# A mixture-of-experts layer whose experts are taken in an order ranked on the chip

## The chip, the cores and the metric

The kernel runs on one core of a Trainium2 chip. The metric is the device time of one execution in microseconds (us), as the median of several runs; lower is better.

## The reference, cut to what matters

One encoder layer for 256 tokens of width 1024. A first half (convolution branch, differential attention, output projection) makes the residual stream `x`; the second half, where the change lies, sends each token to 4 of 32 experts:

```python
h2 = rms_norm(x, norm2_g[l]) * (1.0 + scale2) + shift2
logits = (h2 @ w_router + b_router)            # 256 x 32
top_v, top_i = lax.top_k(logits, 4)
gates = jax.nn.softmax(top_v, axis=-1)
...
gu = xb @ w_gate_up[e] + b_gate_up[e]          # xb: the tokens of expert e, 1024 -> 2 x 1024
g, u = jnp.split(gu, 2, axis=-1)
g = jnp.minimum(g, 7.0); u = jnp.clip(u, -7.0, 7.0)
y = (u + 1.0) * (g * jax.nn.sigmoid(1.702 * g))
return y @ w_down[e] + b_down[e]               # 1024 -> 1024
...
x = x + gate2 * (sum over a token's experts of gate * output)
```

All is float32. An expert has 12 MB of weights, the 32 experts 384 MB; each weight is used once per execution. The experts get 256·4/32 = 32 tokens on average, but unevenly.

## The kernel before

**Places.** The second half is a loop over 32 places `e` (L1010 to L1065); before the change place `e` is expert `e`. An expert's first 64 tokens are its first pass. A second pass takes tokens 65 to 128 of an expert that has more than 64: its parts stand in `tc.If(n > 64)` blocks, with `n` the expert's count, which `count(e)` (L950) loads from the row `cnt` into registers of PE, ACT and DVE. Further passes, for more than 128, stand behind the loop and are skipped with this input.

**One place.** PE runs the gate half (`gate_up(PG, …)`, line L857, 4 weight chunks); then the If with `extra_gate` (L1018); the bias and the up half (4 chunks); the turning of the result and the gathering of the next pair's tokens; the If with `extra_up` (L1038); the adding of earlier outputs into `Y`; the next gate's bias; `down` (L898, 4 chunks); and the If with `extra_down` (L1064). The order in each engine's queue is the order written. DVE's L862 (`gp<-pg`) starts when a gate ends. DVE's L923 runs only in a second pass, in `extra_gate`.

**Tokens.** `pos` holds each token's position within each expert, `ge` its gate weight, `ehot` a one-hot matrix over experts that picks bias rows. `hots` and `extra_hot` (`hx`) turn columns of these into matrices that select tokens. All columns are picked by a constant `e`.

**Weights.** `expert_weights(e)` (L955) issues the loads on SP's queue, one `dma_start` for each chunk of 128x2048 floats (1 MB): 8 of `wgu` and 4 of `wdn` an expert. The chunks go around a ring of 19 buffers (8 + 7 + 4 of three pools), so chunk n waits until PE has finished with chunk n − 19. PE's last use of a chunk comes after the If of its part, since a second pass uses the same chunks: four become free after L1018, four after L1038, four after L1064. SP issues in order, up to 8 weight transfers underway at once.

```python
    pattern = [ringA] * 8 + [ringB] * 7 + [ringW] * 4
...
    def wchunk(src):
        t = wtile()
        nc.sync.dma_start(t, src)
        return t
```

**Place 0.** Weights are issued long ahead of the loop, while the routing is worked out. During place 0's gate the function `turn_gates` (step k = 6 of 8) transposes `ge` on PE (L1003) and copies it to `gT` (L1004).

Of the kernel before, what the change touches and what calls it, by code (L numbers as in the profile page):

```python
# [13 lines left out]
T = 256  # L14
NT = 2
# [16 lines left out]
def hybrid_layer(tc, xT_d, par_d, ada_d, win_d, wout_d, bgu_d, bdn_d, wgu_d, wdn_d, out_d):  # L32
# [771 lines left out]
    def hots(es, name, weight):  # L804
        hot = wk.tile([128, NT, 2, 64], F32, name=name)
        for t in range(NT):
            for i, e in enumerate(es):
                V.tensor_scalar(hot[:, t, i], iota[:, 0:64], pos[:, t, e:e + 1], weight(t, e),
                                op0=OP.is_equal, op1=OP.mult)
        return hot.rearrange("p a b c -> p a (b c)")  # L810

    def gate_hots(es):
        return hots(es, "hotg", lambda t, e: ge[:, t, e:e + 1])
# [29 lines left out]
    def bias(e, g, tag=None):  # L843
        P = ps_e.tile([128, 512], F32, name=tag or ("pg", "pu")[g])
        for n in range(2):
            o = g * 1024 + n * 512
            TE.matmul(P[64 * n:64 * n + 64], ehot[:, e:e + 1].to_broadcast([96, 64]), b3[:, o:o + 512],
                      start=True, stop=False)
        return P
# [53 lines left out]
    def extra_hot(e, b):  # L903
        hot = wk.tile([128, NT, 64], F32, name="hx")
        for t in range(NT):
            V.tensor_scalar(hot[:, t], iota[:, 64 * b:64 * b + 64], pos[:, t, e:e + 1], r2[:, t:t + 1],
                            op0=OP.is_equal, op1=OP.mult)
        return hot

    def extra_gate(e, b, W, hot):  # L910
        xg = more2.rearrange("p (k s) -> p k s", k=KD)
        for q, tag in enumerate(("misc", "pd")):
            px = ps_e.tile([128, 4, 64], F32, name=tag)
            for i in range(4):
                k = 4 * q + i
                for t in range(NT):
                    TE.matmul(px[:, i], xtok[:, t, k * 128:k * 128 + 128], hot[:, t], start=t == 0, stop=t == NT - 1)
            for i in range(4):
                affine(xg[:, 4 * q + i], px[:, i], 4 * q + i)

        hg = more1.rearrange("p (t c s) -> p t c s", t=NT, c=2)
        for t in range(NT):
            V.tensor_scalar(hg[:, t], iota[:, None, 64 * b:64 * b + 64].to_broadcast([128, 2, 64]),  # L923
                            pos[:, t, e:e + 1], ge[:, t, e:e + 1], op0=OP.is_equal, op1=OP.mult)
        act_g(gate_up(bias(e, 0), xg, W), more3)
# [5 lines left out]
    def extra_up(e, W):  # L931
        xg = more2.rearrange("p (k s) -> p k s", k=KD)
        act_u(gate_up(bias(e, 1, "misc"), xg, W), more3, more3)
# [10 lines left out]
    def extra(e, b, W, D):  # L944
        extra_gate(e, b, W[0:4], extra_hot(e, b))
        extra_up(e, W[4:8])
        extra_down(D)

    def count(i, engines=(ET.PE, ET.Activation, ET.DVE)):
        return nc.values_load(cnt[0:1, i:i + 1], engines=engines, min_val=0, max_val=2 * T,  # L950
                              skip_runtime_bounds_check_because="a count of tokens")
# [27 lines left out]
    Y = [ps_y.tile([128, 2, T], F32, name=f"y{i}") for i in range(4)]  # L979
    prep_hot(0)  # L980
# [29 lines left out]
    for e in range(NE):  # L1010
# [160 lines left out]
```

## Time and profile before

| | |
|---|---|
| median of 3 runs | 1149.2 us (1148.97 to 1150.4) |
| the profiled execution's own time | 1154.69 us |
| its span in the profile | 1152.9 us |
| PE busy | 1074.8 us (93% of the span) |
| DVE, ACT, POOL busy | 337.9 (29%), 161.0 (14%), 24.8 (2%) |

The profile shows one execution, taken by the hardware profiler. Its page cuts the span into 40 slices of 28.8 us. A clock column gives the granted TensorE clock as a share of 2.4 GHz. "Busy" PE means that a matmul is in the array, not that the array is at its peak. A window row gives for one stretch its length, each engine's busy time with its count of instructions (PE, PE's weight loads, DVE, ACT, POOL), the mean granted clock, the DMA engines' busy share and the GB/s moved. A timeline row gives start, duration, engine, line, operation, what it writes <- what it reads, and in brackets the idle time before it with what ended that. SPq is SP's queue of DMA issues.

### The profile page before, as it was taken

How to read it: one execution, taken by the hardware profiler on the slowest of the kernel's cores; microseconds unless marked ns; L12 is line 12 of the kernel's file. 1: busy time of each engine (PE TensorE's matmuls, PEld its weight loads, DVE VectorE, ACT ScalarE, POOL GpSimd, SP SyncE). 2: the span in 40 equal slices, each digit the busy share in tenths (PEclk: the TensorE clock that was granted, in tenths of full speed). 3: DMA queues.
4: the chain of work that ended last, by engine and by line, in shares of the span. 5: the costliest groups of instructions: out<-in, count | busy, mean ns of one | idle time of the engine just before them, and what ended most of it. 6: DMA issues, size and time to landing. Idle time of an engine off the chain costs nothing. (4 is left out here: it accounts for less than half of the span.)

```text
span 1152.9 us, 13876 instructions
## 1 busy us (share of the span) xinstructions
PE 1074.8 (93%) x5404; PEld 489.7 (42%) x5409; DVE 337.9 (29%) x837; ACT 161.0 (14%) x333; POOL 24.8 (2%) x54
## 2 busy tenths in 40 slices
PE   8999999999999999999999999998988888898996
PEld 6645774444433444433444444443333333333333
DVE  4897762222221222221222222221222221211212
ACT  2343521101110010100101111010101000000100
POOL 0160000000000000000000000000000000000000
PEclk9999999999999999999999999999999999999999
DMA  9999589999997999977999999999999999999994
GB/s 371 395 349 358 211 308 421 418 419 420 418 422 291 396 419 420 420 296 290 408 420 419 420 418 419 420 419 420 419 420 420 420 420 419 419 420 420 419 405 152
DMA packets 65428, 448.59 MB, mean 389 GB/s; under 512 B 7744, under 2 KB 7744, under 8 KB 11808
## 3 DMA queue, kind: packets, MB, share of 16 engines
q1 hardware_dynamic: 63856, 445.27, 94.4%
q8 instruction: 83, 1.36, 0.5%
q0 software_dynamic: 1456, 1.69, 0.5%
q14 instruction: 33, 0.27, 0.1%
HBM read 444.33 MB, written 1.05 MB: 386 GB/s over the span
## 5 line engine op out<-in xcount | busy, mean ns | idle before, releaser
L857 PE MATMUL pu<-w,xg 128*64 128x512 f32 x1024 | 233.5, 596 | 20.1 <-DMA w<-in_wgu_dram 19.9
L857 PE MATMUL pg<-w,xg 128*64 128x512 f32 x1024 | 232.5, 597 | 12.6 <-DMA w<-in_wgu_dram 7.4
L898 PE MATMUL pd<-w,yT 128*64 128x512 f32 x992 | 218.1, 592 | 0.0
L857 PEld LDWEIGHTS pg<-w,xg 128*64 128x64 f32 x1024 | 79.4, 136 | 159.8 <-issue 139.0
L857 PEld LDWEIGHTS pu<-w,xg 128*64 128x64 f32 x1024 | 76.4, 136 | 154.8 <-issue 99.5
L898 PEld LDWEIGHTS pd<-w,yT 128*64 128x64 f32 x992 | 69.6, 137 | 127.9 <-issue 124.2
L862 DVE TENSOR_SCALAR gp<-pg 128x512 f32<-128x512 f32 x34 | 23.5, 692 | 218.7 <-PE pg L857 218.7
L1061 DVE COPY o<-pd 64x512 f32<-64x512 f32 x31 | 21.2, 683 | 226.4 <-PE pd L898 226.4
L871 DVE TENSOR_SCALAR gp<-pu 128x512 f32<-128x512 f32 x32 | 22.1, 692 | 169.8 <-issue 164.2
L840 PE MATMUL y<-s,o 128*128 128x256 f32 x256 | 64.0, 390 | 4.0
L824 PEld LDWEIGHTS misc<-hot,xtok 128*128 128x128 f32 x496 | 57.9, 192 | 12.4 <-issue 12.2
L824 PE MATMUL misc<-hot,xtok 128*128 128x128 f32 x496 | 62.1, 278 | 0.0
L217 DVE SCALAR_TENSOR_TENSOR w<-w,crow 128x1024 f32<-128x1024 f32 x48 | 56.8, 1220 | 12.7 <-DMA w<-in_ada_dram 12.7
L840 PEld LDWEIGHTS y<-s,o 128*128 128x128 f32 x256 | 45.7, 189 | 20.9 <-issue 16.1
L1063 ACT ACTIVATE o<-pd 64x512 f32<-64x512 f32 x31 | 18.4, 594 | 256.2 <-DVE o L1061 256.2
L865 ACT ACTIVATE sg<-gp 128x512 f32<-128x512 f32 x32 | 20.2, 631 | 234.5 <-DVE gp L862 234.5
L404 PE MATMUL pq<-w,hT 128*128 128x512 f32 x96 | 42.7, 596 | 0.0
L882 ACT ACTIVATE yT<-pu 128x256 f32<-128x256 f32 x32 | 12.3, 384 | 175.0 <-PEq L1038 164.7
L800 ACT ACTIVATE xg<-misc,modT,a 128x128 f32<-128x128 f32 x62 | 28.4, 458 | 43.2 <-DVE xg L802 43.2
L270 PE MATMUL cv<-hT,w 128*128 128x256 f32 x128 | 30.2, 397 | 3.4 <-DMA w<-in_win_dram 3.4
L643 PE MATMUL pq<-mixT,w 128*128 128x256 f32 x128 | 29.3, 382 | 1.5 <-DVE xT L699 1.5
L802 DVE TENSOR_SCALAR xg<-misc,a,modT 128x128 f32<-128x128 f32 x62 | 25.2, 406 | 18.3 <-ACT xg L800 16.4
(308 smaller groups left out, 680.1 us busy)
## 6 DMA issues: line engine op xcount, KB each, us to landing
w<-in_wgu_dram SPq DMA_DIRECT2D x256, 1024.0 KB, 19.9
w<-in_wdn_dram SPq DMA_DIRECT2D x124, 1024.0 KB, 19.9
w<-in_ada_dram SPq DMA_DIRECT2D x24, 1024.0 KB, 13.8
w<-in_win_dram SPq DMA_DIRECT2D x10, 1024.0 KB, 12.7
w<-in_wout_dram SPq DMA_DIRECT2D x4, 1024.0 KB, 10.9
w<-in_wdn_dram SPq DMA_DIRECT2D x8, 512.0 KB, 14.4
w<-pad POOLq DMA_DIRECT2D x32, 35.5 KB, 6.2
xT<-in_xT_dram SPq DMA_DIRECT2D x4, 256.0 KB, 9.9
```

Of the source, the lines that this page charges most:

```text
L217: V.scalar_tensor_tensor(w, w, 1.0, crow, op0=OP.mult, op1=OP.mult, accum_out=modT[:, s, 2 * q + i:2 * q + i + 1])
L270: TE.matmul(pcv[j][:, g], WI[0, q][:, o:o + 128], hT[:, k], start=k == 0 and g == 0, stop=k == KD - 1, skip_group_check=True)
L404: TE.matmul(PQ[w, t], hT[:, k, t * 128:t * 128 + 128], WI[1 + w, k // 4][:, (k % 4) * 512:(k % 4) * 512 + 512], start=k == 0, stop=k == KD ...
L643: TE.matmul(po4[d // 2][:, d % 2], WO[i][k // 2][:, o:o + 128], mixT[:, 4 * i + k], start=first and k == 0 and d % 2 == 0, stop=last and k ...
L800: A.activation(dst, src, AF.Identity, scale=a2[:, k:k + 1], bias=sh2[:, k:k + 1])
L802: V.tensor_scalar(dst, src, a2[:, k:k + 1], sh2[:, k:k + 1], op0=OP.mult, op1=OP.add)
L824: TE.matmul(px[:, i], xtok[:, t, k * 128:k * 128 + 128], PP[p][:, t], start=t == 0, stop=t == NT - 1)
L840: TE.matmul(Y[d // 2][:, d % 2], O[p][:, d * 128:d * 128 + 128], S[p].rearrange("p a b -> p (a b)"), start=False, stop=False, skip_group_c ...
L857: TE.matmul(P[64 * n:64 * n + 64], xg[:, k], W[k // 2][:, o:o + 512], start=False, stop=k == KD - 1)
L862: V.tensor_scalar(gp, P, 7.0, None, op0=OP.min)
L871: V.tensor_scalar(y, P, -7.0, 7.0, op0=OP.max, op1=OP.min)
L898: TE.matmul(P[64 * n:64 * n + 64], yT[:, j, half * 64:half * 64 + 64], down_part(W, f, n), start=f == 0, stop=f == 7)
```

## The change

Experts 0 and 1 stay at places 0 and 1. For the others, `ranks` (DVE) ranks the experts by count (ties by number), and a fixed table `rho`, made by POOL, says which rank a place takes: places 2 to 17 take ranks 2 to 17 (fewest tokens first), places 18, 20, 22, … 30 take ranks 31, 30, 29, … 25 (most tokens first), and places 19, 21, … 31 take ranks 18, 19, … 24. The one-hot matrix `place` holds the result. During place 0's gate `reorder` takes the place of `turn_gates`: at k = 3, 5 and 7 PE multiplies with `place`, and DVE copies out `ids` (the expert number and the count of each place), `posp` and `gep` (positions and gates with columns in the new order); `ehotp` is the matrix for the biases. From place 2 on, all use these, and `expert_weights` loads the expert's number from `ids` into a register of SP and addresses the weights with it. `count` reads from `ids`.

```diff
+    countb = cp.tile([128, NE], F32, name="countb")
+    A.activation(countb, pp[:, 2], AF.Copy)
...
+    def order_setup():
+        rho = more3[:, 0:NE]
+        G.iota(rho, pattern=[[1, NE]], base=0, channel_multiplier=0, allow_small_or_imprecise_dtypes=True)
+        tail = rho[:, 18:NE].rearrange("p (n two) -> p n two", two=2)
+        G.iota(tail[:, :, 0], pattern=[[-1, 7]], base=31, channel_multiplier=0, allow_small_or_imprecise_dtypes=True)
+        G.iota(tail[:, :, 1], pattern=[[1, 7]], base=18, channel_multiplier=0, allow_small_or_imprecise_dtypes=True)
+        return rho
+
+    def ranks():
+
+        key = more3[:, NE:2 * NE]
+        V.scalar_tensor_tensor(key, countb, 32.0, iota[:, 0:NE], op0=OP.mult, op1=OP.add)
+        V.tensor_scalar(key[:, 0:2], iota[:, 0:2], -30000.0, None, op0=OP.add)
+        junk = more3[:, 2 * NE:3 * NE]
+        own = more3[:, 4 * NE:4 * NE + 2]
+        V.scalar_tensor_tensor(junk[:96], key[:96], 1.0, ehot, op0=OP.mult, op1=OP.mult, accum_out=own[:96, 0:1])
+        V.scalar_tensor_tensor(junk[:96], key[:96], own[:96, 0:1], ones32[:96], op0=OP.is_lt, op1=OP.mult,
+                               accum_out=own[:96, 1:2])
+        V.tensor_scalar(place, rho[:96], own[:96, 1:2], None, op0=OP.is_equal)
+        V.tensor_copy(ehotp, place)
+
+        V.scalar_tensor_tensor(junk[:32], countb[:32], 1.0, ehot[:32], op0=OP.mult, op1=OP.mult, accum_out=num[:, 1:2])
+
+    def reorder(k):
+
+        if k == 3:
+            PT[0] = ps_e.tile([128, 512], F32, name="pu")
+            for t in range(NT):
+                TE.transpose(PT[0][0:32, t * 128:t * 128 + 128], pos[:, t], identf)
+            for i in range(2):
+                TE.matmul(PT[0][0:1, 256 + 32 * i:288 + 32 * i], num[:, i:i + 1], place[:32], start=True, stop=True)
+            V.tensor_copy(ids, PT[0][0:1, 256:320])
+            V.tensor_scalar(counts[:, NE + 1:], PT[0][0:1, 319:320], 64.0, counts[:, NE:NE + 1], op0=OP.add, op1=OP.max)
+            V.tensor_copy(cnt[:, NE + 1:], counts[:, NE + 1:])
+            V.tensor_copy(gT, PT[0][0:32, 0:256])
+        if k == 5:
+            px = ps_e.tile([128, 512], F32, name="pu")
+            for t in range(NT):
+                TE.matmul(px[:, 32 * t:32 * t + 32], gT[:, t * 128:t * 128 + 128], place[:32], start=True, stop=True)
+            V.tensor_copy(posp.rearrange("p t e -> p (t e)"), px[:, 0:64])
+            for t in range(NT):
+                TE.transpose(px[0:32, 256 + t * 128:256 + t * 128 + 128], ge[:, t], identf)
+            V.tensor_copy(gT, px[0:32, 256:512])
+        if k == 7:
...
+            V.tensor_copy(gep.rearrange("p t e -> p (t e)"), px[:, 0:64])
...
     def expert_weights(e, again=False):
-        gu = [wchunk(wgu_d[e, c // 4, c % 4]) for c in range(8)]
-        if e < NE - 1 or again:
-            return gu, [wchunk(wdn_d[e, c]) for c in range(4)]
+        last = e == NE - 1 and not again
+        if e > 1 and not again:
+            e = nc.values_load(ids[0:1, e:e + 1], engines=(ET.SP,), min_val=0, max_val=NE - 1,
+                               skip_runtime_bounds_check_because="the number of an expert")
+
+        def of(src, *i):
+            if isinstance(e, int):
+                return src[(e,) + i]
+            return src[(bass.ds(e, 1),) + i].rearrange("o p n -> (o p) n")
+
+        gu = [wchunk(of(wgu_d, c // 4, c % 4)) for c in range(8)]
...
+    ranks()
     V.tensor_reduce(counts[:, NE:NE + 1], counts[:, :NE], axis=AX.X, op=OP.max)
-    V.tensor_scalar(counts[:, NE + 1:], counts[:, NE - 1:NE], 64.0, counts[:, NE:NE + 1], op0=OP.add, op1=OP.max)
-    V.tensor_copy(cnt, counts)
+    V.tensor_copy(cnt[:, :NE + 1], counts[:, :NE + 1])
...
-    def turn_gates(k):
-        if k == 6:
-            pgt = ps_e.tile([128, T], F32, name="pu")
-            for t in range(NT):
-                TE.transpose(pgt[0:32, t * 128:t * 128 + 128], ge[:, t], identf)
-            V.tensor_copy(gT, pgt[0:32])
...
-        sg = act_g(gate_up(PG, xg, W[0:4], turn_gates if e == 0 else turned_out if last else None))
-        n = count(e)
+        sg = act_g(gate_up(PG, xg, W[0:4], reorder if e == 0 else turned_out if last else None))
+        n = count(e) if e < 2 else count(NE + e, row=ids)
```

`hots`, `extra_hot`, `bias` and `extra_gate` pick `pos`, `ge`, `ehot` for places 0 and 1 and `posp`, `gep`, `ehotp` after that. The loops, the ring and the If blocks stay as they are.

PE in the gate of place 0, before: `pg` is the gate's result, `w` a weight chunk, `pu` a scratch result.

```order
L857 MATMUL pg<-w,xg 64x512 x12
L1003 MATMUL pu<-identf,ge 32x128 x2
L857 MATMUL pg<-w,xg 64x512 x4
L950 TENSOR_LOAD cnt
L1018 COMPARE_AND_BRANCH
```

The same place now (L919 is the gate's line, `s` the tile of `gT`):

```order
L919 MATMUL pg<-w,xg 64x512 x6
L826 MATMUL pu<-identf,pos 32x128 x2
L828 MATMUL pu<-place,num 1x32 x2
L919 MATMUL pg<-w,xg 64x512 x4
L836 MATMUL pu<-place,s 128x32 x2
L839 MATMUL pu<-identf,ge 32x128 x2
L919 MATMUL pg<-w,xg 64x512 x4
L844 MATMUL pu<-place,s 128x32 x2
L919 MATMUL pg<-w,xg 64x512 x2
L1015 TENSOR_LOAD cnt
L1090 COMPARE_AND_BRANCH
```

Five groups of small products and transposes stand where one stood; those on `s` need DVE copies from the block before.

SP where place 2's first weights are issued (behind the last three down chunks of place 1), before:

```order
L687 DMA w<-in_wdn_dram 128x2048 x3
L1064 UNCONDITIONAL_BRANCH
L687 DMA w<-in_wgu_dram 128x2048 x3
L1018 UNCONDITIONAL_BRANCH
L687 DMA w<-in_wgu_dram 128x2048 x4
```

And now:

```order
L687 DMA w<-in_wdn_dram 128x2048 x3
L1023 TENSOR_LOAD ids
L687 ISA
L687 DMA w<-in_wgu_dram 128x2048
L1136 UNCONDITIONAL_BRANCH
L687 ISA
L687 DMA w<-in_wgu_dram 128x2048
L687 ISA
L687 DMA w<-in_wgu_dram 128x2048
L687 ISA
L687 DMA w<-in_wgu_dram 128x2048
L1090 UNCONDITIONAL_BRANCH
```

Each issue has a register operation (ISA) ahead of it, and the first of each place a register load from `ids`. The number and order of the transfers are the same.

DVE ahead of the softmax of the gates, now; the seven rows from L809 to L819 are new:

```order
L863 TENSOR_SCALAR xg<-pd,a_237,modT 128x128 x2
L809 SCALAR_TENSOR_TENSOR more_1377<-countb,iota 128x32
L810 TENSOR_SCALAR more_1377<-iota 128x2
L813 SCALAR_TENSOR_TENSOR more_1377<-more_1377,ehot 96x32
L814 SCALAR_TENSOR_TENSOR more_1377<-more_1377 96x32
L816 TENSOR_SCALAR place<-more_1377 96x32
L817 CAST ehotp<-place 96x32
L819 SCALAR_TENSOR_TENSOR more_1377,num<-countb,ehot 32x32
L1065 TENSOR_REDUCE counts<-counts 1x1
```

They stand between the copies of the gathered tokens (`xg`) and the counts, so the gates `ge` and `hx` come after them.

## Rows read from the trace of the kernel before

**Rows 1.** The page, part 2: GB/s in 40 slices of 28.8 us
```profile
GB/s 371 395 349 358 211 308 421 418 419 420 418 422 291 396 419 420 420 296 290 408 420 419 420 418 419 420 419 420 419 420 420 420 420 419 419 420 420 419 405 152
```
**Rows 2.** Windows: start:end, length, engines' busy us, clock, DMA share, GB/s
```profile
200.00:350.00 150.00, 144.66 (x724) 63.20 (x721) 35.09 (x80) 16.31 (x34) 0.00 (x0) 0.99 1.01 420
...
350.00:400.00 50.00, 47.00 (x230) 19.80 (x228) 8.36 (x19) 4.10 (x8) 0.00 (x0) 1.00 0.82 332
...
500.00:570.00 70.00, 64.62 (x315) 27.93 (x312) 12.28 (x26) 5.78 (x12) 0.00 (x0) 0.98 0.78 310
...
570.00:775.00 205.00, 200.13 (x996) 87.82 (x994) 47.77 (x109) 21.16 (x43) 0.00 (x0) 1.00 1.01 419
...
775.00:1100.00 325.00, 289.61 (x1372) 110.23 (x1368) 67.11 (x155) 28.80 (x58) 0.95 (x1) 1.00 1.01 420
```
**Rows 3.** Line L923, only in the second pass of a place: ns min/median/max, starts
```profile
L923 DVE TENSOR_SCALAR more<-iota,pos,ge x4: 339/342/346, 318.7 to 487.5; 128x128 f32<-128x128 f32 x4
```
**Rows 4.** Timeline, DVE: start, us, line (L862 starts when a gate ends)
```profile
313.92 0.69 DVE L862 TENSOR_SCALAR gp<-pg 128x512 f32<-128x512 f32 x1 [5.87 <-PE pg L857]
...
375.54 0.69 DVE L862 TENSOR_SCALAR gp<-pg 128x512 f32<-128x512 f32 x1 [9.64 <-PE pg L857]
...
482.48 0.69 DVE L862 TENSOR_SCALAR gp<-pg 128x512 f32<-128x512 f32 x1 [5.86 <-PE pg L857]
...
543.90 0.69 DVE L862 TENSOR_SCALAR gp<-pg 128x512 f32<-128x512 f32 x1 [9.64 <-PE pg L857]
...
757.08 0.69 DVE L862 TENSOR_SCALAR gp<-pg 128x512 f32<-128x512 f32 x1 [5.87 <-PE pg L857]
...
815.16 0.69 DVE L862 TENSOR_SCALAR gp<-pg 128x512 f32<-128x512 f32 x1 [6.77 <-PE pg L857]
...
1087.99 0.69 DVE L862 TENSOR_SCALAR gp<-pg 128x512 f32<-128x512 f32 x1 [7.33 <-PE pg L857]
```
**Rows 5.** Timeline of PE in the second pass of place 10, and a 2 us window
```profile
506.10 0.64 PE L847 MATMUL misc<-b,ehot 96*64 96x512 bf16 x2 [2.74 <-ACT xg L800]
...
340.00:342.00 2.00, 2.00 (x6) 0.57 (x4) 0.00 (x0) 0.00 (x0) 0.00 (x0) 0.50 1.01 422
```
**Rows 6.** A window, SP's weight issues and PE around place 0
```profile
154.61:180.76 26.15, 24.79 (x155) 15.86 (x155) 12.61 (x56) 8.00 (x16) 0.50 (x1) 0.93 1.00 390
...
154.18 0.33 SPq L687 DMA_DIRECT2D w<-in_wgu_dram  x1
...
154.61 2.20 SPq L687 DMA_DIRECT2D w<-in_wdn_dram  x4
...
156.91 24.18 SPq L687 DMA_DIRECT2D w<-in_wgu_dram  x8
...
190.82 0.33 SPq L687 DMA_DIRECT2D w<-in_wdn_dram  x1
...
201.91 7.09 PE L857 MATMUL pg<-w,xg 128*64 128x512 f32 x32 [0.16 <-PEq L1064]
```
**Rows 7.** Timeline of DVE and PE in the gate of place 0
```profile
165.28 0.41 DVE L765 SCALAR_TENSOR_TENSOR L<-pc,rr,rbias 128x32 f32<-128x32 f32 x2 [1.16 <-PE pc L747]
...
176.40 0.53 DVE L906 TENSOR_SCALAR hx<-iota,pos,rr 128x64 f32<-128x64 f32 x2
...
178.80 0.41 DVE L1004 COPY s<-pu 32x256 f32<-32x256 f32 x1 [1.88 <-PE pu L1003]
...
173.12 5.32 PE L857 MATMUL pg<-w,xg 128*64 128x512 f32 x24
...
178.37 0.39 PE L1003 MATMUL pu<-identf,ge 128*32 128x128 f32 x2
```
**Rows 8.** Lines L950 and L687 on SP's queue: ns min/median/max; landing in us
```profile
L950 SPq TENSOR_LOAD <-cnt x2: 423/449/475, 1145.5 to 1146.3; - x2
...
L687 SPq DMA_DIRECT2D w<-in_wgu_dram x256: 327/328/863, 109.5 to 1106.2; - x128
...
DMA to landing us min/median/max: 4.7/19.9/22.5
```

More of the change, by code (lines that the diff above doesn't have):

```diff
@@ new lines, in reorder @@
+    def reorder(k):
[18 more added lines that the diff above has]
+        if k == 7:
+            px = ps_e.tile([128, 512], F32, name="pu")
+            for t in range(NT):
+                TE.matmul(px[:, 32 * t:32 * t + 32], gT[:, t * 128:t * 128 + 128], place[:32], start=True, stop=True)
+            V.tensor_copy(gep.rearrange("p t e -> p (t e)"), px[:, 0:64])
@@ L797, in hybrid_layer @@
+    PT = {}
+    cnt = cp.tile([1, NE + 2], I32, name="cnt")
+    ids = cp.tile([1, 2 * NE], I32, name="ids")
+    place = cp.tile([96, NE], F32, name="place")
+    ehotp = cp.tile([96, NE], BF, name="ehotp")
+    num = cp.tile([NE, 2], F32, name="num")
+    posp = cp.tile([128, NT, NE], F32, name="posp")
+    gep = cp.tile([128, NT, NE], F32, name="gep")
     XG, S, O, PP = {}, {}, {}, {}
@@ L841, in scatter, with bias @@
                       start=False, stop=False, skip_group_check=True)
-    def bias(e, g, tag=None):
+    def bias(e, g, tag=None, hot=None):
+        hot = (ehot if e < 2 else ehotp) if hot is None else hot
         P = ps_e.tile([128, 512], F32, name=tag or ("pg", "pu")[g])
@@ L900, in down, with extra_hot, extra_gate @@
         return P
-    def extra_hot(e, b):
+    def extra_hot(e, b, ps=None):
+        ps = (pos if e < 2 else posp) if ps is None else ps
         hot = wk.tile([128, NT, 64], F32, name="hx")
         for t in range(NT):
-            V.tensor_scalar(hot[:, t], iota[:, 64 * b:64 * b + 64], pos[:, t, e:e + 1], r2[:, t:t + 1],
+            V.tensor_scalar(hot[:, t], iota[:, 64 * b:64 * b + 64], ps[:, t, e:e + 1], r2[:, t:t + 1],
                             op0=OP.is_equal, op1=OP.mult)
         return hot
-    def extra_gate(e, b, W, hot):
+    def extra_gate(e, b, W, hot, by=None):
+        ps, gs_, eb = by or (posp, gep, None)
         xg = more2.rearrange("p (k s) -> p k s", k=KD)
@@ L923, in extra_gate @@
             V.tensor_scalar(hg[:, t], iota[:, None, 64 * b:64 * b + 64].to_broadcast([128, 2, 64]),
-                            pos[:, t, e:e + 1], ge[:, t, e:e + 1], op0=OP.is_equal, op1=OP.mult)
-        act_g(gate_up(bias(e, 0), xg, W), more3)
+                            ps[:, t, e:e + 1], gs_[:, t, e:e + 1], op0=OP.is_equal, op1=OP.mult)
+        act_g(gate_up(bias(e, 0, None, eb), xg, W), more3)
         px = ps_e.tile([128, NT, 128], F32, name="misc")
@@ L929, in extra_gate, with extra_up @@
         A.activation(more1.rearrange("p (a b) -> p a b", a=NT), px, AF.Copy)
-    def extra_up(e, W):
+    def extra_up(e, W, eb=None):
         xg = more2.rearrange("p (k s) -> p k s", k=KD)
-        act_u(gate_up(bias(e, 1, "misc"), xg, W), more3, more3)
+        act_u(gate_up(bias(e, 1, "misc", eb), xg, W), more3, more3)
     def extra_down(W):
@@ L944, in extra, with count @@
     def extra(e, b, W, D):
-        extra_gate(e, b, W[0:4], extra_hot(e, b))
-        extra_up(e, W[4:8])
+        extra_gate(e, b, W[0:4], extra_hot(e, b, pos), (pos, ge, ehot))
+        extra_up(e, W[4:8], ehot)
         extra_down(D)
-    def count(i, engines=(ET.PE, ET.Activation, ET.DVE)):
-        return nc.values_load(cnt[0:1, i:i + 1], engines=engines, min_val=0, max_val=2 * T,
+    def count(i, engines=(ET.PE, ET.Activation, ET.DVE), row=None):
+        row = cnt if row is None else row
+        return nc.values_load(row[0:1, i:i + 1], engines=engines, min_val=0, max_val=2 * T,
                               skip_runtime_bounds_check_because="a count of tokens")
@@ L955, in expert_weights @@
     def expert_weights(e, again=False):
-        gu = [wchunk(wgu_d[e, c // 4, c % 4]) for c in range(8)]
-        if e < NE - 1 or again:
-            return gu, [wchunk(wdn_d[e, c]) for c in range(4)]
+        last = e == NE - 1 and not again
[7 more added lines that the diff above has]
+        gu = [wchunk(of(wgu_d, c // 4, c % 4)) for c in range(8)]
+        if not last:
+            return gu, [wchunk(of(wdn_d, c)) for c in range(4)]
         for n in range(2):
```

16 lines of the change are left out of this document (10 added, 6 removed).

## The prediction

> **What bounds the kernel now.** I read the bytes first. Outside the start and end, the slices of the page hold 418 to 421 GB/s with four gaps [rows 1]. Two lie ahead of the experts (211 and 308); the windows cut the other two out: 420 GB/s on either side, 332 in 350 to 400 us, 310 in 500 to 570 us [rows 2]. Against 420 the transfers stand still for 50·(1 − 332/420) = 10.5 us and 70·(1 − 310/420) = 18.3 us, 28.8 us in all. Each gap follows one of the second passes (65th token and on), which happen twice: line L923 has four instances, two to a pass, from 318.7 to 487.5 us [rows 3].
>
> Then PE. A gate ends where DVE's L862 starts, so I took a place's length from these starts [rows 4]. From 543.90 to 757.08 us lie eight places: **26.65 us** each, with no bytes missing; PE sets this pace. From 815.16 to 1087.99 lie nine: **30.31 us** each, the pace of 12 MB of weights at 420 GB/s [rows 2]. So without a second pass PE is 3.66 us a place faster than the weights. A pass costs 375.54 − 313.92 − 26.65 = 34.97 at the first and 543.90 − 482.48 − 26.65 = 34.77 at the second [rows 4], mean **34.87 us**.
>
> The two limits meet in the ring of 19 chunks. A pass puts PE behind; the transfers run on until the ring is full, then stand until PE releases. PE catches up 3.66 us a place. How far behind PE can be with the transfers still running: carry the late pace back from 815.16 by nine places, 815.16 − 9·30.31 = 542.37, or ten to place 11, 512.06. Place 11's gate ended at 543.90, with the ring full: **31.8 us**. By this line the second pass stopped the transfers (543.90 − 375.54) − 5·30.31 = 16.8 us, against 18.3 by bytes. With the first's 10.5 that is 27.3 to 28.8. This stand-still is the kernel's loss: it ends paced by the weights, so every microsecond of it is in the time.
>
> **The change part by part.** *1. The passes move to 18 and 20.* The line without any stand-still puts gate 5 at 815.16 − 16·30.31 − 27.3 = 302.9; it ended at 313.92, so PE is then 11.0 behind. With no pass there it has caught up three places later (11.0/3.66), and from place 8 to 18 PE waits for weights. That wastes PE's advantage: it can't run ahead of bytes that have not come. Now place by place:
> - gate 18 ends at 815.16 − 3·30.31 − 27.3 = **696.9**, PE 0 behind;
> - gate 19 (first pass) 696.9 + 26.65 + 34.87 = 758.4, 31.2 behind: just within 31.8, no stand-still;
> - gate 20 at 785.1, 27.5 behind;
> - gate 21 (second pass) **846.6**, 27.5 + 31.2 = 58.8 behind, which is 27.0 over the limit: the transfers stand **27.0 us**;
> - from there 31.8 − 3.66 a place: back at 0 at place 29.7.
>
> Gate 30 by the weights is 815.16 + 9·30.31 − 27.3 + 27.0 = 1087.65; by PE it is 846.6 + 9·26.65 = 1086.45. The later one counts: **1087.65 against 1087.99** before [rows 4]. The order moves the stand-still; it doesn't remove it. One stall of 27.0 replaces two of 27.3, because the two places from one pass to the next give back 7.3 us; the ring would need 27.0/3.66 = 7.4 places more. Term: −0.3; with 28.8 for the old stalls the weights' line falls to 1086.15 and PE's to 1084.95, so −1.8.
>
> Against this stands that the bounding resource changes in the trace: 26.65 us a place after a pass, 30.31 later [rows 4], and the new order puts passes where weights bind. By the Trainium skill ("Perfetto Trace Analysis", section Optimization Strategy), where the most contended engine changes over time, interleaving the regimes may improve performance; by that rule the sum would be rival A's, by the rows it is the −0.3 above, and the rows decide since they show the ring's limit.
>
> *2. Ranking and turned tables in place 0.* DVE gains seven operations ahead of the softmax. None is over 128x32; two such took 0.41 at L765 [rows 7], 0.2 each, 1.5 in all. hx ends at 176.40 + 0.53 + 1.5 = 178.4, and the four copies after it (ids, two of the count, gT) take 3·0.2 + 0.41 = 1.0: 179.4. On PE the second added block (k = 5) needs gT. It stands after five sixths of the group of 24 [rows 7], 173.12 + 4.43 = 177.55, and the first block's two transposes (0.39 the pair) and two tiny products bring that to 178.3, so PE waits 1.1. With the first block's 0.75 and two more small pairs, half of 0.39 each, place 0 is later by **2.2 us**; the gate's transposes only move, from k = 6 to k = 5. Ends: 1.2, were the copies to beat PE; 4, if the next copy stalls PE as well.
>
> Is it covered? In 154.61 to 180.76 us the core moved 390 GB/s [rows 6], 10.2 MB; issued were 12 chunks of 1.05 MB (one chunk just before 154.61, four and seven of the eight within), 12.6 MB. The 2.4 MB left last 5.7 us, to 186.5. A new chunk needs some 2.2 us before bytes flow (4.7 least from issue to landing [rows 8] less 2.5 for 1.05 MB), so releases may come 3.5 us later than the first one at 180.8; by the same count 3.5 at 190.82 and 2.4 at 201.91 [rows 6]. The delay of 2.2 is below the least, 2.4: cost **0**, ends 0 and 1.6 (at 4). If that cover were gone, it would cost one for one.
>
> *3. Weights by register.* On SP, 30 register loads at 0.423 to 0.475 and a register operation before each of 360 transfers (bounds: 0 and the 0.33 of an issue) [rows 8]. A chunk takes 2.5 us; SP's 0.33 + 0.33 leaves room, and SP mostly waits for landings of 19.9 us median [rows 8]. Only where the transfers have stood still is SP on the path: 0 to 1.3 us over some four restarts, take 0.3.
>
> *4. Counts from ids, countb on ACT, iotas on POOL.* The loads into PE, ACT and DVE stay one a place; countb is one small copy ahead of the first gather; POOL is idle through the experts [rows 2]. 0.
>
> **Sum:** −0.3 + 0 + 0.3 + 0 = 0 on the profiled 1154.69 us; at the median 1149.2, **1149.2**. The profiled execution is 5.5 us longer than the median, all rows come from it, and I assume this offset stays. The parts' bounds are −1.8 to +0, 0 to +1.6, 0 to +1.3.
>
> **The rivals.** A measurement here tells 0.2%, 2.3 us, from no change.
> - *A, the ring swallows both passes.* All 27 to 29 us come back, 1121.9. Against: from gate 18 to 30 PE needs 12·26.65 + 2·34.87 = 389.6, the weights 12·30.31 = 363.7, so even an endless ring would leave PE as the bound 26 us later. For it: only if PE's 26.65 had slack. Chance 0.03.
> - *B, a smaller gain.* The old stalls were 28.8 as the bytes say, the limit is a little above 31.8, and PE instead of the weights sets the end, so the wait for the last weights shrinks: −1.8, and up to half of a place's 3.66 more: 1145.5. For: the two counts of the second stall differ by 1.5. Chance 0.17.
> - *C, passes dearer late (slower).* From gate 18 on, both paths carry the passes: PE pays each in full, the stand-still too. In a pass the granted clock stood at 0.50 (1.2 GHz) in 340 to 342 us, and PE had waited 2.74 us for ACT's gather at 506.10 [rows 5]. If a pass that follows ten places of waits for weights runs more in the low clock, each extra microsecond counts twice. It decides from about 1.2 us a pass (2.3 over the two); at 2 a pass: 1153. Chance 0.10.
> - *D, place 0 is later than the cover (slower).* From 2.4 us on, one for one: at 7 us, 1149.2 + 4.6 = 1153.8. Chance 0.10.
> - *E, SP's register work shows.* If a register operation blocks SP until an earlier transfer is handed on, or landings set the pace differently, each of some 360 costs; 0.02 us each is 7 us: 1156. Chance 0.05.
> - That the change doesn't do what it says: passes at other places. Then gains as in A or none; contained in A and the forecast.
>
> **How the numbers follow.** Forecast (within 2.3 us) 0.55; A and B make faster 0.20; C, D and E slower 0.25. The range reaches from B's middle, with 1 us beyond, to C and D: 1144.5 to 1154.0; A and E lie outside.
>
> **What would show it.** L923's successor starts near 700 and 789 us, none before. GB/s stays at 420 from 200 to about 790 us; one dip between 790 and 860, with about 27 us missing. Gate ends: 18 near 697, 21 near 847, 30 near 1087.7. PE waits for weights in places 8 to 18 and not in 21 to 29. Place 0's gate ends at 182 to 184. The prediction is wrong if the transfers stand still for less than 20 us after place 20 (A), a pass costs over 36.1 us (C), bytes dip before 250 us (D), or the line between stalls is under 415 GB/s (E).

## The result and the profile after

The changed kernel took **1156.85 us** (median of 4 runs, 1155.43 to 1157.53) against 1149.8 for the kernel before (4 runs): ratio 1.0058, 95% interval 1.0041 to 1.0076. A second comparison of 12 runs with 35 (below, e2) gave 1.0040, 1.0024 to 1.0055. So it is slower, by 4 to 7 us, where no change was forecast.

The profile hardly shows it: its execution took 1155.43 us, against 1154.69 for the profiled one of before. The page's span and bytes, in 40 slices of 28.8 us (they answer to [rows 1]):

```profile
span 1153.7 us, 14695 instructions
...
GB/s 370 394 346 389 208 326 412 410 418 418 418 417 419 418 419 419 417 420 418 419 418 419 418 418 420 405 384 345 146 378 417 417 418 418 418 418 417 418 417 174
```

The two gaps behind places 5 and 10 are gone, and one large gap stands behind places 18 and 20. The windows of the same profile (columns as in [rows 2]):

```profile
200.00:350.00 150.00, 146.49 (x723) 61.97 (x720) 34.21 (x79) 14.99 (x30) 0.00 (x0) 1.00 1.01 417
...
570.00:700.00 130.00, 116.11 (x560) 46.33 (x557) 25.93 (x59) 11.49 (x23) 0.00 (x0) 1.00 1.01 419
700.00:775.00 75.00, 69.78 (x348) 30.38 (x349) 15.10 (x35) 7.71 (x17) 0.00 (x0) 0.98 0.97 399
775.00:820.00 45.00, 42.10 (x214) 18.83 (x208) 10.61 (x24) 5.04 (x11) 0.00 (x0) 0.96 0.68 274
820.00:870.00 50.00, 47.36 (x234) 19.68 (x234) 8.36 (x19) 4.48 (x9) 0.00 (x0) 1.00 0.81 326
```

Against 418 the transfers stood still for 75·(1 − 399/418) + 45·(1 − 274/418) + 50·(1 − 326/418) = 3.4 + 15.5 + 11.0 = 29.9 us; before it was 28.8 in two pieces. The second passes' line, then DVE's first row after a gate (the gates of places 0, 18, 19, 20, 21 and 30; L924 is what L862 was in [rows 4]):

```profile
L987 DVE TENSOR_SCALAR more<-iota,posp,gep x4: 336/340/343, 702.7 to 790.8; 128x128 f32<-128x128 f32 x4
```

```profile
180.81 0.69 DVE L924 TENSOR_SCALAR gp<-pg 128x512 f32<-128x512 f32 x1 [0.79 <-PE pg L919]
...
697.88 0.69 DVE L924 TENSOR_SCALAR gp<-pg 128x512 f32<-128x512 f32 x1 [7.51 <-PE pg L919]
...
759.00 0.69 DVE L924 TENSOR_SCALAR gp<-pg 128x512 f32<-128x512 f32 x1 [9.64 <-PE pg L919]
785.73 0.69 DVE L924 TENSOR_SCALAR gp<-pg 128x512 f32<-128x512 f32 x1 [5.86 <-PE pg L919]
...
847.17 0.69 DVE L924 TENSOR_SCALAR gp<-pg 128x512 f32<-128x512 f32 x1 [9.64 <-PE pg L919]
...
1088.98 0.69 DVE L924 TENSOR_SCALAR gp<-pg 128x512 f32<-128x512 f32 x1 [6.70 <-PE pg L919]
```

Place by place the sum holds: gate 18 at 697.88 (forecast 696.9), 19 at 759.00 (758.4), 20 at 785.73 (785.1), 21 at 847.17 (846.6), 30 at 1088.98 (1087.65). What does not hold is the last step, from the profiled execution to the median of the runs: the kernel before runs 5 us faster than its profile, the changed one's medians lie within 1.6 us of its profiles (1155.43 here, 1156.84 in e2). The experiments ask why.

### The profile page after: what moved, and what is told of

Read it like the earlier page. It is cut to its first block, busy times and chain, and to the rows that moved or that the text cites. A ratio compares the mean times of both kernels' runs of the same rounds, so it can differ in the third digit from the quotient of the medians.

```text
span 1153.7 us, 14695 instructions
## 1 busy us (share of the span) xinstructions
PE 1075.3 (93%) x5423; PEld 490.0 (42%) x5423; DVE 340.3 (29%) x852; ACT 160.9 (14%) x334; POOL 25.4 (2%) x59
## 5 line engine op out<-in xcount | busy, mean ns | idle before, releaser
L919 PE MATMUL pu<-w,xg 128*64 128x512 f32 x1024 | 233.3, 596 | 19.2 <-DMA w<-in_wgu_dram 19.2
L919 PE MATMUL pg<-w,xg 128*64 128x512 f32 x1024 | 233.1, 597 | 13.3 <-DMA w<-in_wgu_dram 8.4
L919 PEld LDWEIGHTS pg<-w,xg 128*64 128x64 f32 x1024 | 79.9, 136 | 159.1 <-issue 138.2
L919 PEld LDWEIGHTS pu<-w,xg 128*64 128x64 f32 x1024 | 76.5, 136 | 153.7 <-issue 101.4
L924 DVE TENSOR_SCALAR gp<-pg 128x512 f32<-128x512 f32 x34 | 23.5, 692 | 218.7 <-PE pg L919 218.7
```

The source lines that it names most:

```text
L919: TE.matmul(P[64 * n:64 * n + 64], xg[:, k], W[k // 2][:, o:o + 512], start=False, stop=k == KD - 1)
L924: V.tensor_scalar(gp, P, 7.0, None, op0=OP.min)
```

## The experiments

In the runs below, "passes" are second passes, and a time is a median; ratios are to the kernel before on the same chip, with 95% intervals. 5 to 12 runs stand behind each.

### Profiles again, the order alone, the registers alone (e1 to e4)

e1 and e2 are the two kernels unchanged. e3 is the kernel before with the order of the change as constants:

```diff
+    EX = [0, 1, 22, 2, 20, 14, 6, 8, 27, 4, 3, 25, 31, 19, 30, 9, 7, 18, 10, 24, 5, 23, 17, 16, 11, 21, 29, 13, 28, 26, 12, 15]
...
-        gu = [wchunk(wgu_d[e, c // 4, c % 4]) for c in range(8)]
+        gu = [wchunk(wgu_d[EX[e], c // 4, c % 4]) for c in range(8)]
...
-        n = count(e)
+        n = count(EX[e])
```

(and so for `pos`, `ge`, `ehot`, `wdn_d`). e4 is the changed kernel with a key and a table that put expert e at place e:

```diff
-        V.scalar_tensor_tensor(key, countb, 32.0, iota[:, 0:NE], op0=OP.mult, op1=OP.add)
+        V.scalar_tensor_tensor(key, countb, 0.0, iota[:, 0:NE], op0=OP.mult, op1=OP.add)
...
-        G.iota(tail[:, :, 0], pattern=[[-1, 7]], base=31, channel_multiplier=0, allow_small_or_imprecise_dtypes=True)
-        G.iota(tail[:, :, 1], pattern=[[1, 7]], base=18, channel_multiplier=0, allow_small_or_imprecise_dtypes=True)
+        G.iota(tail[:, :, 0], pattern=[[2, 7]], base=18, channel_multiplier=0, allow_small_or_imprecise_dtypes=True)
+        G.iota(tail[:, :, 1], pattern=[[2, 7]], base=19, channel_multiplier=0, allow_small_or_imprecise_dtypes=True)
```

> The kernel before, unchanged, profiled and timed beside the others. Theory R (register addressing: each weight transfer addressed by a register reaches the engines a little later or slower): ratio 1.000, and the profile's gate 30 near 1083 rather than 1088 us, since the first profile was 5 us over the runs. Theory P (places: the new order of passes costs the time): the same ratio. Theory N (the first profile of before was one of a slower spell of the weights, and only that hid the difference): GB/s between the stand-stills above 420 in this profile, 421 to 423.

> The changed kernel, unchanged, on the same chip as the others of this call. All theories: 1.004 to 1.008 again. Under theory R the weights' line between stand-stills (places 9 to 17) is 0.1 to 0.3 us a place longer than in the kernel before on this chip; under theory P it is the same.

> The order of the change with every place's expert a constant of the program: no ranking, no turned tables, no register. Passes at places 18 and 20. Theory R: ratio 0.998 to 1.001 (the time of before). Theory P: 1.004 to 1.008 (the time of the change).

> The changed kernel with a key and a table that give place e expert e again: all the ranking, turning and register addressing, but the passes at 5 and 10 as before. Theory R: 1.004 to 1.008 or more (1.010), since it is bound by the weights in more places. Theory P: 0.999 to 1.002.

Measured: e1 1151.9, 1.0015 (0.9997 to 1.0033), the same kernel; e2 1155.24, 1.0040 (1.0024 to 1.0055); e3 1153.25, **1.0027** (1.0011 to 1.0044); e4 1154.73, **1.0034** (1.0017 to 1.0051). Neither theory: the order alone costs about 3 us, the rest of the change alone about 4, and both together not 7 but 4 to 5. Theory N missed too, since e1's profile has 420 GB/s like the first. But e1's profile took 1149.96, and its passes 33.3 and 33.1 us in place of 34.97 and 34.77. The clock shows why. Three windows of the first profile of before (columns as in [rows 2], the third figure from the end is the granted clock):

```profile
160.00:166.00 6.00, 6.00 (x48) 4.61 (x47) 2.65 (x17) 1.23 (x3) 0.00 (x0) 0.72 1.02 367
336.00:342.00 6.00, 4.29 (x14) 1.67 (x16) 0.64 (x2) 0.92 (x2) 0.00 (x0) 0.74 1.01 422
504.00:510.00 6.00, 3.90 (x12) 1.63 (x14) 1.03 (x3) 0.92 (x2) 0.00 (x0) 0.72 0.70 289
```

and the same places of the program, 3 to 5 us earlier, in a later profile of the same work, e10's (below), which took 1147.63:

```profile
154.00:166.00 12.00, 10.97 (x86) 8.44 (x85) 7.74 (x38) 3.92 (x8) 0.49 (x1) 1.00 1.01 393
333.00:339.00 6.00, 4.73 (x24) 2.09 (x26) 0.41 (x1) 0.74 (x2) 0.00 (x0) 1.00 1.01 422
500.00:506.00 6.00, 5.04 (x26) 2.19 (x28) 0.41 (x1) 0.46 (x1) 0.00 (x0) 1.00 0.48 199
```

A mean clock of 0.72 over 6 us says that part of it ran at 0.50 (1.2 GHz), and loses 6·0.28 = 1.7 us. The profile that the prediction was made from held three such falls, one ahead of place 0 and one at the end of the wait of 2.74 us of each pass [rows 5], 5.1 us of PE's time in all, close to the 5.5 us by which it lay over its median. The two in the passes are 3.4 us of this; what the first did to place 0 isn't shown, since in e1 gate 0 also ended late (179.71), with no fall ahead of it. The changed kernel's profile held three as well, in place 0 and in both passes:

```profile
193.00:199.00 6.00, 6.00 (x22) 2.44 (x22) 0.00 (x0) 0.45 (x1) 0.00 (x0) 0.72 1.01 416
720.00:726.00 6.00, 4.51 (x16) 1.85 (x18) 0.41 (x2) 0.92 (x2) 0.00 (x0) 0.72 1.02 423
808.00:814.00 6.00, 4.66 (x16) 1.91 (x18) 0.41 (x1) 0.81 (x2) 0.00 (x0) 0.72 0.00 0
```

yet that execution was not slow for its kernel. Either the changed kernel nearly always has falls in its passes, or a part of what is late in the old order doesn't count in the new one. The next runs take these apart.

### The wait in the pass, the registers, another place (e5 to e8, e11, e12)

e5 and e6 give the up half of a pass another PSUM tile, in the kernel before and in the changed one:

```diff
-        act_u(gate_up(bias(e, 1, "misc"), xg, W), more3, more3)
+        act_u(gate_up(bias(e, 1, "pd"), xg, W), more3, more3)
```

e12 and e11 do the same with "pu" in place of "pd".

e7 is the changed kernel with constant addresses, e8 the changed kernel with the two fullest experts at places 10 and 20:

```diff
-            e = nc.values_load(ids[0:1, e:e + 1], engines=(ET.SP,), min_val=0, max_val=NE - 1,
-                               skip_runtime_bounds_check_because="the number of an expert")
+            e = EX[e]
```

```diff
-        tail = rho[:, 18:NE].rearrange("p (n two) -> p n two", two=2)
...
+        for a, n, r in ((10, 1, 31), (11, 9, 10), (20, 1, 30), (21, 11, 19)):
+            G.iota(rho[:, a:a + n], pattern=[[1, n]], base=r, channel_multiplier=0,
+                   allow_small_or_imprecise_dtypes=True)
```

> The kernel before, but the second pass's up half sums in another PSUM tile, so that PE needn't wait 2.74 us for ACT's and DVE's copies of the gathered tokens. Theory C (the clock falls to 1.2 GHz in that wait in some executions and makes a pass 34.8 instead of 33.1 us): every pass 30.4 us, granted clock 1.00 throughout it, both stand-stills shorter; 2*2.74 plus on average one to two times 1.7: 1141 to 1144 us, ratio 0.992 to 0.995, and the runs lie closer together (under 5 us from lowest to highest instead of 8). Rival (the clock falls in a pass whatever PE does there): ratio 0.994 to 0.996, 1.2 GHz still seen in a pass, spread as before.

> The changed kernel with the same edit. Theory C: passes of 30.4 us, about 9 us off the changed kernel (1155.2): 1146 to 1148. If dear passes alone made the change slower (they came in both passes of both its profiles), it equals the kernel before with this edit within 1 us; if registers and place 0 do (theory R), it stays 2.5 to 4 us above it.

> The changed kernel with ranking, turned tables and its order, but the weights' addresses are constants of the program (SP has no register work). Theory R (register-addressed transfers stream at 418 instead of 420 GB/s, 0.14 us a place over the 18 places bound by weights): 2 to 3 us below the changed kernel, 1152 to 1153.5, with 420 GB/s in the slices. Rival (place 0's added work starves the ring): the same time as the changed kernel, 1154.5 to 1156, and the dip below 415 GB/s near 200 us stays.

> The changed kernel with another table: highest rank at place 10, second highest at 20, the others in rising order. Ring theory (a pass makes PE 31 us late, nine places at 3.66 give it back, so both fit the ring one after the other): no stand-still over 3 us, weights bind to the end, 27 to 30 us off the changed kernel: 1125 to 1128. Rival (the stand-still comes with any pass, whatever its place): two stand-stills of 10 to 17 us, about 1150 to 1155.

> The changed kernel, the second pass's up half in the PSUM tile of the turned result instead: PE waits about 1.0 us instead of 2.74 for it, and the places without a pass keep 26.65 us. Theory C (the clock falls in the long wait): passes of 31.4 us without 1.2 GHz, 2*(1.7 + 1.7) = 6.8 us off: 1148 to 1149. Rival (the clock falls anyway): passes of 33 us, 3.4 us off: 1151.5 to 1152.5.

> The same edit in the kernel before. Theory C: passes of 31.4 us, 3.4 us off for the shorter wait and 0.9 to 1.7 for the clock: 1145.5 to 1147, and the runs from lowest to highest within 5 us instead of 8. It then lies 2 to 2.5 us under the changed kernel with the same edit (alignment alone), not 4.5. Rival: 3.4 us off and the spread as before.

**The wait.** e11's pass shows the bias waiting 1.08 us in place of 2.74, and the clock at 1.00 there:

```profile
719.96 0.41 PE L909 MATMUL pu<-b,ehotp 96*64 96x512 bf16 x2 [1.08 <-DVE yT L945]
```

```profile
718.00:724.00 6.00, 4.92 (x28) 2.32 (x29) 1.15 (x3) 1.30 (x3) 0.00 (x0) 1.00 1.01 419
```

Its passes took 31.43 us both, and it ran 1148.95 (0.9994; 0.9980 to 1.0008), 6.3 under e2 (5.3 by the ratios, since the chips differ; theory C expected 6.8). Over all profiles of this study the fall came in 11 of 24 passes with the wait of 2.74 us, and in none of 14 with a shorter one or none. By the Trainium skill ("TensorE: Matmul & The Clock Gate", section Part 1: The HAM clock gate) the gate follows how busy PE has been, and the same kernel shows it differently from run to run; the trace agrees: both passes of the first profile had a fall of 1.7 us, neither pass of e1's did. In the old order 4 of 10 such passes had it, at 18 and 20 seven of 12; too few to call different.

**But the difference stays.** e12 ran **1144.88** (0.9960; 0.9945 to 0.9974), 4.1 us under e11, where theory C expected 2 to 2.5, and a little under its own 1145.5. With no fall seen in any pass the new order is about as far behind as before. So dear passes explain little of the difference, and e6's nearness to e5 (1149.01 to 1148.33) misled: "pd" made every place without a pass 0.26 us longer, 26.9 us, as `down`, which sums in that tile, now started 0.47 us after the next gate's bias in place of 0.24, and e5 missed its 1141 to 1144. The old order paid more for this: by the ratios e5 is 1.7 us above e12, and e6 1.8 under e11. That it does so because PE binds it in more places is argued, not shown.

**Registers.** e7 ran 1155.72 (1.0040; 1.0026 to 1.0054), the time of the changed kernel, at the same 418 GB/s. Theory R is out: the 764 instructions by which the two profiles differ, nearly all of them SP's, cost nothing that these runs show, good to some 2.4 us either way.

**Place.** e8 ran **1128.67** (0.9803; 0.9783 to 0.9824), just over the 1125 to 1128 of the ring theory. Its bytes have no stand-still, only slices of 403 to 406 behind the passes:

```profile
GB/s 371 397 343 382 228 299 411 416 420 418 418 419 417 419 419 418 418 419 404 419 417 418 418 418 418 418 420 418 406 403 417 419 418 418 419 418 418 418 415 157
```

This shows the ring's part: with ten places between the passes, and the second 11 ahead of the end, the stand-still is gone; with two, as in the change, it is all there. The page that the prediction quoted against itself (the Trainium skill, "Perfetto Trace Analysis", Optimization Strategy) is right at 10 and 20 and not at 18 and 20.

### A late place 0, in both orders (e13, e14)

What was left: what does the end hang from? In the old order PE is the bound from place 0 up to the place where the ring is full, so lateness in place 0 should come out at the end. In the new one it is the weights' line up to place 18. e13 adds 18 transposes to place 0 of the kernel before, e14 the same to e3:

```diff
             for t in range(NT):
                 TE.transpose(pgt[0:32, t * 128:t * 128 + 128], ge[:, t], identf)
+            for t in range(18):
+                TE.transpose(pgt[0:32, t % 2 * 128:t % 2 * 128 + 128], ge[:, t % 2], identf)
```

> The kernel before with 18 more transposes on PE at step 6 of place 0's gate (0.195 us each, 3.5 us; they only repeat what is there). Theory H (in the old order the end hangs from PE's chain from place 0 on, so anything that is late there counts in full): 3.5 us slower, ratio 1.0030 (1.002 to 1.004). Rival (place 0 has slack in both orders): ratio 1.000 to 1.001.

> The same 18 transposes in the order of the change with constants (1.0027 of the kernel before without them). Theory H (in the new order the end hangs from the weights' line up to place 18, which has some slack in place 0): 0 to 1.2 us more, ratio 1.0027 to 1.0038, and gate 18 ends within 1.2 us of 695.9. Rival (place 0 counts in full here too): 3.5 us more, ratio 1.0055 to 1.006, gate 18 near 699.4.

Measured: e13 1155.95, **1.0031** (1.0009 to 1.0052); e14 1153.56, **1.0019** (1.0005 to 1.0032), no more than e3's 1.0027. The same 3.5 us of PE show as 3.6 us (1.0 to 6.0) in the old order and as −0.9 in the new, good to some 2.5 either way: theory H. The whole 3.5 us is ruled out in the new order; a part of it is not. Two gates of e3 and then of e14, places 0 and 18:

```profile
177.24 0.69 DVE L863 TENSOR_SCALAR gp<-pg 128x512 f32<-128x512 f32 x1 [1.47 <-PE pg L858]
...
695.92 0.69 DVE L863 TENSOR_SCALAR gp<-pg 128x512 f32<-128x512 f32 x1 [8.14 <-PE pg L858]
```

```profile
180.70 0.69 DVE L863 TENSOR_SCALAR gp<-pg 128x512 f32<-128x512 f32 x1 [1.47 <-PE pg L858]
...
697.97 0.69 DVE L863 TENSOR_SCALAR gp<-pg 128x512 f32<-128x512 f32 x1 [6.87 <-PE pg L858]
```

In these two executions a part does come through. e14's profile also had a fall in place 0, so its gate 1 ended 5.3 us after e3's (210.78 and 205.52). Gate 18 moved by 2.1, more than the 1.2 expected, and the time, less 1.7 for the one fall that each had in a pass, by 3.0 (1150.1 to 1153.1). The profiles of the old order with the wait of 2.74 us lie within 0.8 us of one line: 970.3 us, plus the end of gate 0, plus 1.7 for each fall from there to the end of the second pass. From e1 (179.71, no fall: 1149.96) it gives 1147.6 for e10 (177.30, none; its time was 1147.63), 1154.4 for the first profile (180.68, two; 1154.69), 1154.2 for e4 (182.18, one; 1154.96) and 1156.5 for e13 (181.06, one in a pass and one twice as long in place 0; 1155.88). In the new order the same lateness shows less. e9 (below) had the latest gate 0 of all,

```profile
184.50 0.69 DVE L924 TENSOR_SCALAR gp<-pg 128x512 f32<-128x512 f32 x1 [0.79 <-PE pg L919]
...
699.09 0.69 DVE L924 TENSOR_SCALAR gp<-pg 128x512 f32<-128x512 f32 x1 [7.21 <-PE pg L919]
```

and took 1152.81 without a fall in a pass. Less 1.7 for each fall in a pass, e3 (gate 0 at 177.24) took 1150.1, the changed kernel 1152.0 (180.81), e14 1153.1 (180.70) and e2 1153.4 (180.41). The last three had a fall in place 0 too. So of the lateness of place 0 the old order passes on all, the new one, in these profiles, between a third and three fifths (e9 against e3: 2.7 of 7.3 us; e14 against e3: 3.0 of 5.3).

### Where the ring starts (e9, e10, e15 to e17)

Between the stand-stills the page's slices show 418 GB/s in the kernels so far that have the new tables, e7 without registers among them, and 420 in those without. The new small tiles move the ring. By the sizes of the tiles as the kernels allocate them (the profile shows no addresses), 12 of the 19 buffers started 384 bytes past a multiple of 512 (all seven others at 480), and now all 19 start at 480. e9 puts one tile into another's spare end (12 buffers at 448):

```diff
-    counts = cp.tile([1, NE + 2], F32, name="counts")
+    counts2 = cp.tile([NE, NE + 4], F32, name="counts")
+    counts, num = counts2[0:1, 0:NE + 2], counts2[:, NE + 2:]
...
-    num = cp.tile([NE, 2], F32, name="num")
```

e10 puts 32 bytes ahead of them in the kernel before (12 at 416):

```diff
+    shift = cp.tile([128, 8], F32, name="shift")
+    V.memset(shift, 0.0)
```

e15 is e8 with e11's short wait (19 buffers at 480); e16 and e17 are e15 with all 19 at 448 and at 416, by such tiles on both sides of SBUF.

> The changed kernel with one small tile (num) put into the spare end of another, so that 12 of the ring's 19 buffers start 32 bytes lower: at a multiple of 64 bytes again, as in the kernel before; the seven others lie off it in all kernels so far. Alignment theory: 420 instead of 418 GB/s in the slices, 0.13 us a place over 18 places bound by weights, 2 to 2.5 us below the changed kernel (1152.7 to 1153.5). Rival (the ranking or something else in the change slows the weights): 418 GB/s and 1155 to 1156.

> The kernel before with 32 bytes put ahead of those 12 buffers, nothing else. Alignment theory: 418 GB/s, 0.13 us a place over the 20 places bound by weights behind the passes: 2 to 3 us slower, ratio 1.002 to 1.003. Rival: 420 GB/s and ratio 0.999 to 1.001.

> The changed kernel with the passes at 10 and 20 and the short wait (up half of a second pass in the PSUM tile of the turned result). Weights bind throughout in the run with 10 and 20 alone (1128.7), where three slices still showed 403 to 406 GB/s. Ring theory: each pass is 1.7 us shorter, PE is at most 28 us behind, the three slices rise to 418: 1 to 3 us off, 1126 to 1127.7. Rival (those slices have another cause): 1128.3 to 1129.

> The same with all 19 buffers of the ring at multiples of 64 bytes (in the run before this all 19 lie 32 bytes off). The run with 12 buffers of the old order moved off showed 420 GB/s and no clear loss, so alignment should do nothing: the same time within 0.5 us. Rival (the 418 GB/s of the changed kernel's runs against 420 come from the address of the ring all the same): 420 GB/s, 2 to 4 us less, since all 31 places are bound by weights here.

> The run with the aligned ring (1124.8), all 19 buffers now at 416 bytes past a multiple of 512, so 32 bytes off a multiple of 64; in the run before the aligned one they stood at 480 and took 1128.7, in the aligned one at 448. Theory 64 (what counts is a start at a multiple of 64 bytes): 1128.0 to 1129.0 and 418 GB/s. Rival 480 (only a start 32 bytes ahead of a multiple of 512 is slow, which would fit the run with 12 buffers of the kernel before at 416, where no loss was seen): 1124.3 to 1125.3 and 419 to 420 GB/s. If neither: another thing that moved with the tiles.

Measured: e9 1154.29 (1.0045; 1.0027 to 1.0062), not clearly under e2; e10 1150.54 (1.0012; 0.9994 to 1.0030), no clear loss, at 420 GB/s; both too small to decide. e15 1128.69 (0.9810; 0.9785 to 0.9834): the short wait gave nothing where weights bind, against its theory. e16 **1124.80** (0.9765; 0.9743 to 0.9787) and e17 **1124.63** (0.9765; 0.9740 to 0.9789): 4 us less for 32 or 64 bytes, and no run of e16 or e17 (1123.98 to 1127.19) reaches the fastest of e15 (1128.02). The bytes of e15 and then e17:

```profile
GB/s 370 394 345 392 222 310 414 413 418 418 418 418 418 418 419 418 418 420 413 418 418 417 418 418 418 418 419 419 406 404 417 419 418 417 418 419 417 419 413 149
```

```profile
GB/s 371 396 358 390 213 313 412 405 420 420 420 420 420 420 420 421 420 420 417 420 420 420 420 420 419 421 421 420 408 408 419 421 420 419 420 420 420 421 411 147
```

So the theory of multiples of 64 falls (416 is none, and is fast), and of the three starts tried for the whole ring only the one 32 bytes ahead of a multiple of 512 is slow, by some 0.4%. This also fits e10. e17 is the fastest version found, 27 us under the kernel before.

## Why the prediction was wrong

**Right: the passes and the ring.** The order moves the stand-still and doesn't remove it: forecast 27.0 us in one piece, measured 29.9 by bytes, 28.8 before. 3.4 of the 29.9 stand in the window of the first pass, which was forecast at "just within 31.8, no stand-still". Gates 18 to 21 came within 1.0 us, gate 30 within 1.3, and between the two profiled executions the whole difference is +0.7 where 0 was forecast. e8 confirms the ring from the other side. Rival A is out for this order: some 27 us do come back, but only from a spacing that this change doesn't have.

**Wrong: "The profiled execution is 5.5 us longer than the median, all rows come from it, and I assume this offset stays."** This step failed, and with it the sizes that were read from that one late execution: 34.87 us for a pass and 27.3 for the old stalls. Its gate 0 ended at 180.68 where e10's ended at 177.30, and each of its passes held a fall of 1.7 us. In the old order PE's chain from place 0 carries such lateness to the end (e13: 3.5 us added, 3.6 found), so an execution without it is 5 to 7 us faster (e1's profile 1149.96, e10's 1147.63). In the new order PE waits for weights from place 8 to 18 anyway, so an early place 0 gives only a part of it back. The prediction had the fact in hand: "That wastes PE's advantage: it can't run ahead of bytes that have not come." It used it for the stand-still and not for the offset. The gates of e10, which has no fall from place 0 to 30 (shown are places 0, 5, 6, 10, 11, 21 and 30), and gate 30 of e3 show the size:

```profile
177.30 0.69 DVE L864 TENSOR_SCALAR gp<-pg 128x512 f32<-128x512 f32 x1 [1.47 <-PE pg L859]
...
310.49 0.69 DVE L864 TENSOR_SCALAR gp<-pg 128x512 f32<-128x512 f32 x1 [5.87 <-PE pg L859]
...
370.40 0.69 DVE L864 TENSOR_SCALAR gp<-pg 128x512 f32<-128x512 f32 x1 [9.64 <-PE pg L859]
...
477.35 0.69 DVE L864 TENSOR_SCALAR gp<-pg 128x512 f32<-128x512 f32 x1 [5.87 <-PE pg L859]
...
537.09 0.69 DVE L864 TENSOR_SCALAR gp<-pg 128x512 f32<-128x512 f32 x1 [9.64 <-PE pg L859]
...
807.84 0.69 DVE L864 TENSOR_SCALAR gp<-pg 128x512 f32<-128x512 f32 x1 [6.76 <-PE pg L859]
...
1080.91 0.69 DVE L864 TENSOR_SCALAR gp<-pg 128x512 f32<-128x512 f32 x1 [6.77 <-PE pg L859]
```

```profile
1084.99 0.69 DVE L863 TENSOR_SCALAR gp<-pg 128x512 f32<-128x512 f32 x1 [6.84 <-PE pg L858]
```

Here a pass takes 33.26 and 33.09 us. With a pass of 33.18 and all else as the prediction had it, its own sum puts PE 55.4 us behind at gate 21, which is 23.6 over the limit in place of 27.0, and gate 30 at 815.16 + 9·30.31 − 27.3 + 23.6 = 1084.25. That is 3.3 us later than e10's 1080.91. e3, whose gate 0 ended as early (177.24), measured 1084.99, with one fall of 1.7 in a pass. So the mechanism of the ring was right, and the rows were not those of a usual execution. Over 12 runs e3 puts the size of this at 1.0027 of the kernel before.

**Too small: "cost 0" for place 0.** The delay was sized well: with the new work the gate of place 0 ended at 179.5 to 184.5 us in eleven profiles, without it (and without the extra transposes of e13 and e14) at 177.2 to 180.7 in six; the means, 181.4 and 179.0, are 2.4 apart where 2.2 was forecast. But bytes are missing in 200 to 230 us. The rows are, in this order, of the changed kernel, of e2, of e7, of e13 (without that work, but with a late place 0) and of e3 (without either):

```profile
200.00:230.00 30.00, 29.23 (x146) 11.56 (x144) 7.34 (x17) 3.50 (x7) 0.00 (x0) 1.00 1.00 410
```

```profile
200.00:230.00 30.00, 29.23 (x146) 11.45 (x143) 6.29 (x15) 2.91 (x6) 0.00 (x0) 1.00 0.95 389
```

```profile
200.00:230.00 30.00, 29.23 (x146) 11.64 (x144) 7.35 (x17) 3.49 (x7) 0.00 (x0) 1.00 1.01 413
```

```profile
200.00:230.00 30.00, 29.38 (x146) 11.62 (x142) 6.13 (x14) 2.90 (x6) 0.00 (x0) 0.98 0.96 394
```

```profile
200.00:230.00 30.00, 29.39 (x148) 12.00 (x144) 6.12 (x14) 2.90 (x6) 0.00 (x0) 1.00 1.01 418
```

30·(1 − 410/418) = 0.6 and 30·(1 − 389/418) = 2.1 us are missing in the first two, but both had a fall of the clock in place 0, e2 one of twice the length. With the new work and no fall there (e7) it is 30·(1 − 413/418) = 0.4, and without the new work, but with the transposes and a long fall (e13), 30·(1 − 394/420) = 1.9. So the weights did run dry (rival D, at a fraction of its price), by 0.4 us from the new work and by more where a fall came on top. In the old order the same work makes PE's chain late instead (e4, 1.0034). That would be why the two halves of the change don't add up: each makes another one of the two chains late, and the later chain counts.

**The other rivals.** B: the change gave no gain. C: the falls are real, 1.7 us each, but not shown to be more frequent in the new order, and e11 and e12 differ by 4.1 us with none seen in their passes. E: "SP's register work shows" is out by e7. What did slow the line between stalls was no part of the forecast: the ring's start. From e15 to e17 4.06 us went over some 31 places with 19 buffers moved; over 18 places with 12 buffers that is an estimated 4.06·(18/31)·(12/19) = 1.5 us of the changed kernel's loss. e9 could not show it, so it stays an estimate.

**Open.** How often the clock falls in each kernel's unprofiled runs isn't known, so the split of the 4 to 7 us between order, place 0 and ring is good to a microsecond or two. Why gate 0 of the same work ends as early as 177.24 us (e3) or as late as 179.71 (e1) without a fall of the clock is open too.

## What to carry to other kernels

Before a difference between two kernels is read off one profile, ask what was late in that execution and whether the new order would still pass that lateness to the end; a profile's offset over its median belongs to the chain that bounds the kernel, not to the chip. Work that puts the faster of two resources behind is best spread so that the buffer between them can swallow each piece: here ten places apart instead of two gave some 27 us. Adding a small tile can move every large buffer behind it, so look at where those start.

## What the runs showed of the hardware

Transfers of 8 KB a partition into buffers that all start 32 bytes ahead of a multiple of 512 bytes streamed at 418 GB/s, at 64 or 96 bytes ahead of it at 420 (1128.7, 1124.8, 1124.6 us for the kernel). Around the end of a single wait of 2.74 us on PE, behind short products and transposes, the granted clock fell to 0.50 in 11 of 24 cases, at a cost of 1.7 us each time; with a wait of 1.09 us or less, or none, it did so in none of 14. Loading 30 registers on SP and addressing some 360 transfers by them cost nothing that 12 runs can show (1155.72 us with constants, 1155.24 with registers).
